# A row-sum kernel on one core: both halves of a row summed at once in the last 16 rows, fewer last loads, big buffers at a multiple of 1 KB

## Chip, cores, metric

One core of one Trainium2 chip. The metric is the device time of one execution in microseconds; a kernel's time is the median of its runs. The profile's span of the same execution is 1.5 us shorter (161.17 and 159.6 us for before).

## The reference

```python
batch, seq, dim = 32, 512, 1024            # x: float32, 64 MB
return (np.sum(x, axis=-1) / divisor).astype(np.float32)     # divisor = 1024.0
```

16,384 rows of 1024 numbers are read once, each row is summed and scaled: 67.11 MB in, 64 KB out. Each of the 128 partitions has 128 rows.

## The kernel before

The rows come in a few large loads on the SyncE queue into three buffers of 14 rows. VectorE sums most rows with a reduction, ScalarE takes some near the end with an accumulating copy into PSUM. The last 16 rows per partition ("the tail") come in smaller and smaller loads, so that little is left to do when the last byte lands. The last row of all comes in three pieces.

```python
first = [(2, 0), (14, 0)]                      # (rows of a load, of them on ScalarE)
main = [(14, 0)] * 5 + [(14, 4), (12, 5)]
last = [(8, 4), (4, 2), (2, 1)]
bulk = ctx.enter_context(tc.tile_pool(name="bulk", bufs=3))
one = ctx.enter_context(tc.tile_pool(name="one", bufs=1))
# ... small result tiles res0, res, fin, q, r

def act_sum(dst, src, by=1.0):                 # ScalarE
    n = src.shape[-1]
    junk = psum.tile([P, D], F32, name="junk")
    nc.scalar.activation(junk[:, :n], src, COPY, scale=by, accum_out=dst)

def sums(dst, t, rows, on_act):
    d = rows - on_act
    for i in range(d, rows):
        act_sum(dst[:, i : i + 1], t[:, i, :])
    nc.vector.reduce_sum(out=dst[:, :d], in_=t[:, :d, :], axis=AX)
# ... first and main: load, sums(), then one scaling on GpSimd
# ... last: load, sums() into q

c = 704                                        # the row before the last: both engines share it
row = one.tile([P, D], F32, name="row")
load(row, x_last[:, j, :])
act_sum(r, row[:, c:], by=scale)
nc.vector.reduce_sum(out=q[:, j : j + 1], in_=row[:, :c], axis=AX)

a, b = 448, 704                                # the last row: three pieces
# ... pa, pb, pc
load(pa, x_last[:, L - 1, :a])
load(pb, x_last[:, L - 1, a:b])
load(pc[:, : D - b], x_last[:, L - 1, b:])
# ... the results of first and main are stored
act_sum(pc[:, D - b : D - b + 1], pa)
nc.vector.reduce_sum(out=pc[:, D - b + 1 :], in_=pb, axis=AX)
# ... two GpSimd instructions scale the other 15 sums into fin
nc.vector.tensor_scalar(
    out=scaled, in0=pc, scalar1=scale, scalar2=0.0, op0=MULT, op1=ADD, accum_out=fin[:, L - 1 :]
)
tc.keep_in_program_order(nc.sync.dma_start(out=o_last, in_=fin))
```

The last store waits for VectorE, and the queue that issues it first waits until every other transfer, the two earlier result stores included, has landed.

## Time and profile before

| | before |
|---|---|
| time, median of 3 runs | 161.13 us (161.07 to 161.52) |
| span of the profiled run | 159.6 us |
| VectorE / ScalarE / GpSimd busy | 120.9 / 19.7 / 1.4 us |
| bytes over the span | 421 GB/s |
| loads | 16, of 128 KB to 7 MB |
| first load landed / last load landed | 4.94 / 157.54 us |
| final store leaves / lands | 158.18 / 159.59 us |

The first column of a timeline or a chain is the time from the start of the span. A load has landed when its last completion event stands in the trace; an engine that waited for it alone starts 0.02 us later. A handover is the time from the end of one instruction to the start of the next one that needs its result. Nearly all of the span is one unbroken stream of loads: from the first landing to the last one of before the DMA share is 0.99 at 427 GB/s, and in the 2.05 us behind it 0.05.

### The profile page before, as it was taken

Reading aid. Unit: us, or ns where it says so; the run is one execution under the profiler, and the core shown is the slowest. Engines: PE = TensorE matmul, PEld = TensorE weight load, DVE = VectorE, ACT = ScalarE, POOL = GpSimd, SP = SyncE. Lnnn points to the kernel's source line nnn. Section 1 sums busy time; section 2 is a strip of 40 time slices with the busy share of each in tenths; the row PEclk is TensorE's granted clock in tenths of the full one; section 3 lists DMA queues with packets and bytes.
Section 4 is the critical chain, followed back from the end, with each engine's and each line's share of the span. In section 5 each row is a group of like instructions: output and inputs, shape, how many; then the busy total and the mean of one; then the engine's idle time right before and its main releaser. Section 6 shows DMA issues by size and latency. Waiting matters only on the chain.

```text
span 159.6 us, 143 instructions
## 1 busy us (share of the span) xinstructions
DVE 120.9 (76%) x16; ACT 19.7 (12%) x37; POOL 1.4 (1%) x8
## 2 busy tenths in 40 slices
DVE  0500059995999599977999599959995996495985
ACT  3000000000000000000000000000000900490974
POOL 0000000000000000000000000000000000001001
DMA  7999999987999999978999999969999999898994
GB/s 253 470 460 460 460 460 460 431 374 345 460 460 460 460 460 460 417 345 388 460 460 460 460 460 460 402 302 445 460 460 427 394 431 542 357 443 378 413 407 133
DMA packets 2736, 67.18 MB, mean 421 GB/s; under 512 B 688, under 2 KB 1072, under 8 KB 1200
## 3 DMA queue, kind: packets, MB, share of 16 engines
q1 hardware_dynamic: 2736, 67.18, 98.0%
HBM read 67.11 MB, written 0.07 MB: 421 GB/s over the span
## 4 chain that ended last, share of the span: by engine, by line
DMA 76%; DVE 22%; SPq 0%; issue 0%; DVEq 0%
DMA t<-in_x_dram 76%; DVE res L159 20%; DVE q L159 1%; DVE q L184 1%; SPq L148 0%; DVE scaled L207 0%; DVE pc L201 0%; DVEq L207 0%; DVEq L241 0%
## 5 line engine op out<-in xcount | busy, mean ns | idle before, releaser
L159 DVE TENSOR_REDUCE res<-t 128x14 f32<-128x14336 f32 (+3 forms) x9 | 111.2, 12360 | 34.4 <-DMA t<-in_x_dram 34.4
L153 ACT ACTIVATE junk<-t 128x1024 f32<-128x1024 f32 x16 | 16.2, 1013 | 136.0 <-DMA t<-in_x_dram 136.0
L159 DVE TENSOR_REDUCE q<-t 128x4 f32<-128x4096 f32 (+2 forms) x3 | 7.9, 2642 | 2.7 <-DMA t<-in_x_dram 2.7
L153 ACT ACTIVATION_READ_ACCUMULATOR junk<-t 128x1 f32 x16 | 3.0, 187 | 0.0
L168 POOL TENSOR_SCALAR res<-res 128x16 f32<-128x16 f32 (+1 forms) x2 | 0.7, 352 | 145.1 <-DVE res L159 145.1
L153 ACT ACT_TABLE_LOAD x1 | 1.3, 1283 | 1.7 <-PEq L227 1.7
L184 DVE TENSOR_REDUCE q<-row 128x1 f32<-128x704 f32 x1 | 0.9, 885 | 0.0
L207 DVE TENSOR_SCALAR_CACHE_REDUCE scaled<-pc 128x322 f32<-128x322 f32 x1 | 0.5, 489 | 0.1
L153 ACT ACTIVATE junk<-pa 128x448 f32<-128x448 f32 x1 | 0.5, 547 | 0.0
L153 ACT ACTIVATE junk<-row 128x320 f32<-128x320 f32 x1 | 0.4, 442 | 0.1
L201 DVE TENSOR_REDUCE pc<-pb 128x1 f32<-128x256 f32 x1 | 0.4, 420 | 0.0
L202 POOL TENSOR_SCALAR fin<-q 128x14 f32<-128x14 f32 x1 | 0.3, 260 | 10.1 <-DVE q L159 10.1
L203 POOL TENSOR_SCALAR fin<-q,r 128x1 f32<-128x1 f32 x1 | 0.3, 265 | 0.7 <-DVE q L184 0.7
L153 ACT ACTIVATION_READ_ACCUMULATOR junk<-pa 128x1 f32 x1 | 0.2, 187 | 0.0
L153 ACT ACTIVATION_READ_ACCUMULATOR junk<-row 128x1 f32 x1 | 0.2, 186 | 0.0
L227 POOL MEMSET const-bfloat16-1.0<- 128x1 bf16 x1 | 0.1, 101 | 0.0
L227 POOL MEMSET const-uint8-127<- 128x1 uint8 x1 | 0.1, 101 | 0.0
L227 POOL MEMSET const-float32-0.0<- 128x1 f32 x1 | 0.1, 98 | 0.2 <-issue 0.2
L227 POOL MEMSET const-float32-1.0<- 128x1 f32 x1 | 0.1, 99 | 0.0
L207 DVE DVE_READ_ACCUMULATOR scaled<-pc 128x1 f32 x1 | 0.1, 82 | 0.0
## 6 DMA issues: line engine op xcount, KB each, us to landing
t<-in_x_dram SPq DMA_DIRECT2D x7, 7168.0 KB, 35.7
t<-in_x_dram SPq DMA_DIRECT2D x1, 6144.0 KB, 33.3
t<-in_x_dram SPq DMA_DIRECT2D x1, 4096.0 KB, 26.1
t<-in_x_dram SPq DMA_DIRECT2D x2, 1024.0 KB, 18.7
t<-in_x_dram SPq DMA_DIRECT2D x1, 2048.0 KB, 30.5
row<-in_x_dram SPq DMA_DIRECT2D x1, 512.0 KB, 33.2
pa<-in_x_dram SPq DMA_DIRECT2D x1, 224.0 KB, 33.3
pc<-in_x_dram SPq DMA_DIRECT2D x1, 160.0 KB, 33.0
```

The costliest lines, as they stand in the source:

```text
L153: nc.scalar.activation(junk[:, :n], src, COPY, scale=by, accum_out=dst)
L159: nc.vector.reduce_sum(out=dst[:, :d], in_=t[:, :d, :], axis=AX)
L168: nc.gpsimd.tensor_scalar_mul(out=dst, in0=dst, scalar1=scale)
L184: nc.vector.reduce_sum(out=q[:, j : j + 1], in_=row[:, :c], axis=AX)
L201: nc.vector.reduce_sum(out=pc[:, D - b + 1 :], in_=pb, axis=AX)
L202: nc.gpsimd.tensor_scalar_mul(out=fin[:, :j], in0=q[:, :j], scalar1=scale)
L203: nc.gpsimd.tensor_scalar(out=fin[:, j : j + 1], in0=q[:, j : j + 1], scalar1=scale, scalar2=r, op0=MULT, op1=ADD)
L207: nc.vector.tensor_scalar(out=scaled, in0=pc, scalar1=scale, scalar2=0.0, op0=MULT, op1=ADD, accum_out=fin[:, L - 1 :])
L227: nc = _bacc.Bacc("TRN2", target_bir_lowering=False, num_devices=1)
```

## The change

The intent is to shorten what is left at the end. Rows of the tail are summed by VectorE with a two-source instruction that reads the left and the right half of a row together, so that 512 steps do for 1024 columns, and that scales its sum, so that no scaling follows. With quicker sums the tail has fewer loads: 9, 4 and 2 rows and the last row in two pieces. A pad puts the big buffers at byte 17408 in place of 16512, a multiple of 1 KB. In the built programs the small tiles of the tail move too, from multiples of 256 B to multiples of 1 KB.

```diff
-    last = [(8, 4), (4, 2), (2, 1)]
+    last = [(9, 4), (4, 2), (2, 1)]
+    pad = ctx.enter_context(tc.tile_pool(name="pad", bufs=1))
+    pad.tile([P, 224], F32, name="pad")
     bulk = ctx.enter_context(tc.tile_pool(name="bulk", bufs=3))
+    c = 576
+    pa = one.tile([P, 768], F32, name="pa")[:, :c]
+    pb = one.tile([P, D - c + 16], F32, name="pb")[:, : D - c + 2]
+    nc.gpsimd.memset(pb[:, D - c :], 0.0)
+    def dve_mean(dst, src, by=scale):
+        h = src.shape[-1] // 2
+        nc.vector.tensor_tensor_reduce(
+            out=src[:, :h], in0=src[:, :h], in1=src[:, h:], scale=by, scalar=0.0,
+            op0=ADD, op1=ADD, accum_out=dst,
+        )
 ...   (tail: per row dve_mean or act_sum straight into fin)
-    load(row, x_last[:, j, :])
-    load(pa, x_last[:, L - 1, :a])
-    load(pb, x_last[:, L - 1, a:b])
-    load(pc[:, : D - b], x_last[:, L - 1, b:])
+    load(pa, x_last[:, j, :c])
+    load(pb[:, : D - c], x_last[:, j, c:])
 ...
-    act_sum(pc[:, D - b : D - b + 1], pa)
-    nc.vector.reduce_sum(out=pc[:, D - b + 1 :], in_=pb, axis=AX)
-    (three more instructions that scale and add)
+    dve_mean(pb[:, D - c : D - c + 1], pa, by=1.0)
+    dve_mean(fin[:, j:], pb)
```

## The prediction

The sum came to about −0.35 us, 160.8 us: −0.3 for the tail and −0.05 booked for the alignment. The point of 160.85 and the range were set with it. The 85 to 15 for the full rate is the author's own estimate, as no VectorE instruction in the trace of before reads two tensors; the full rate, N/0.96 + 152 ns for N columns, is carried over from the reductions in that trace.

> **What bounds the kernel now.** I first read the chain that ended last, to see whether the time is a stream, an engine or a handover. By line it is 76% loads and 20% the first VectorE reduction, and in order of time its end is this:
>
> ```profile
> 122.55 32.46 DMA t<-in_x_dram
> ...
> 155.04 1.22 DVE q L159
> 156.25 0.01 issue
> 156.27 0.89 DVE q L184
> 157.15 0.39 DVE pc L201
> 157.55 0.04 DVEq L207
> 157.58 0.08 issue
> 157.66 0.49 DVE scaled L207
> ```
>
> The load stream reaches to 155.01 us; then come 3.2 us of VectorE on the last three rows, of which only the last 0.6 us lies behind the last byte (the last piece was issued at 124.49 us and landed 33.0 us later, 157.5 us). So only some tenths of a microsecond at the end are not the stream. The 20% of VectorE inside the chain is no bound: each 14-row reduction of 15.09 us frees a buffer while other loads are queued. The table by stage checks that (columns: span, VectorE, ScalarE and GpSimd busy, clock, DMA share, GB/s):
>
> ```profile
> 40.00:80.00 40.00, 36.31 (x3) 0.00 (x0) 0.00 (x0) 1.00 1.00 434
> 80.00:120.00 40.00, 36.28 (x3) 0.00 (x0) 0.00 (x0) 1.00 1.01 436
> ```
>
> The queues are full, at 434 to 436 GB/s. The timeline of VectorE gives the pace and what the tail does (start, length, instruction, then the idle time before it):
>
> ```profile
> 89.63 15.09 DVE L159 TENSOR_REDUCE res<-t 128x14 f32<-128x14336 f32 x1 [1.85 <-DMA t<-in_x_dram]
> 106.58 15.09 DVE L159 TENSOR_REDUCE res<-t 128x14 f32<-128x14336 f32 x1 [1.86 <-DMA t<-in_x_dram]
> ...
> 138.06 7.62 DVE L159 TENSOR_REDUCE res<-t 128x7 f32<-128x7168 f32 x1 [3.72 <-DMA t<-in_x_dram]
> 147.77 4.42 DVE L159 TENSOR_REDUCE q<-t 128x4 f32<-128x4096 f32 x1 [2.09 <-DMA t<-in_x_dram]
> 152.60 2.29 DVE L159 TENSOR_REDUCE q<-t 128x2 f32<-128x2048 f32 x1 [0.41 <-DMA t<-in_x_dram]
> 155.04 1.22 DVE L159 TENSOR_REDUCE q<-t 128x1 f32<-128x1024 f32 x1 [0.15 <-DMA t<-in_x_dram]
> 156.27 0.89 DVE L184 TENSOR_REDUCE q<-row 128x1 f32<-128x704 f32 x1
> 157.12 0.42 DVE L201 TENSOR_REDUCE pc<-pb 128x1 f32<-128x256 f32 x1
> 157.66 0.49 DVE L207 TENSOR_SCALAR_CACHE_REDUCE scaled<-pc 128x322 f32<-128x322 f32 x1
> ```
>
> Every large reduction waits for its load, so VectorE has slack of 1.85 us per 14 rows. Two landings are 16.95 us apart: 7,340,032 bytes, 433 GB/s. From 156.27 us VectorE runs with almost no gap: there it and the stream are level. Last, what the issuing queue waits for before the final store:
>
> ```profile
> SPq L241 <- DMA out_dram<-res: 1.0, 1, 1.0
> ...
> SPq L210 <- DVE scaled L207: 0.2, 1, 0.2
> ```
>
> It also waits for the two earlier result stores (issued 138.10 and 147.81, landing 19.6 and 10.1 us later: 157.7 and 157.9 us), and only then 0.2 us for VectorE. A faster VectorE alone can win those 0.2 us and no more, unless the stream ends earlier too. The final store (158.18 us) takes 1.4 us and ends the span of 159.6; the measured time is 161.13, 1.5 us more.
>
> [...] In the built programs the three big buffers start at byte 16512 before[...] and at 17408 after (a multiple of 1 KB). The trace of before has no aligned big load to compare. [...] In the trace the reductions [...] 885 ns at 704, 1219 at 1024, 4420 at 4096, which is N/0.96 + 152. [...] No instruction of the trace before has two tensor inputs[...]. [...] I take the full rate as likely, 85 to 15.
>
> **The change part by part.** *Bytes and loads.* The same 67.11 MB; 14 loads for 16: 9 rows for 8, then 4, 2, and the last row in two pieces (576 and 448 columns) for a separate row and three pieces. At the pace above (8 rows took 147.77 − 138.06 = 9.71 us, a row 1.21 us), the landings become: 9 rows 148.97, 4 rows 153.8, 2 rows 156.2 (where the separate row landed), first piece (294,912 B at 433 GB/s, 0.68 us) 156.88, second (229,376 B, 0.53 us) 157.41. That is about 0.1 us earlier than 157.5, for two handovers and a small transfer fewer.
>
> [...]
>
> *VectorE.* Removed: a 4-row, a 2-row and a 1-row reduction, 704, 256 and the scaling of 322 columns: 4.42 + 2.29 + 1.22 + 0.89 + 0.42 + 0.49 = 9.73 us. Added at full rate: eight rows of 512 columns, 512/0.96 + 152 = 685 ns, then 288 columns (452 ns) and 225 (386 ns): 6.3 us, and an accumulator read for each (82 ns in the trace, begun 0.41 us into a 0.49 us instruction, so it lies mostly inside). Of these 3.4 us nearly all are beside the stream: five rows end at 152.4, before 153.8; two at 155.2, before 156.2; one at 156.9. Then the first piece, 156.92 to 157.37, and its sum is handed to the last instruction at about 157.42, level with the second piece. The last one runs 157.46 to 157.85. Before, it ended at 158.15: 0.3 us earlier.
>
> *ScalarE.* 4, 2 and 1 rows as before at 1.04 us each; the last ends near 157.4, inside the above. The short sums of 320 and 448 columns (0.44 and 0.55 us) and the two late GpSimd scalings go: they were hidden. An early fill of the two padding columns (101 ns for such an instruction) is hidden too.
>
> *The store.* The two earlier stores are queued behind all loads. They landed 0.4 us behind the last piece (157.9 against 157.5), so 157.8 now, and the final store leaves at about 157.87 instead of 158.18. Sum: −0.3 us[...].
>
> **Rivals.** *Half rate.* Then a row costs 1024/0.96 + 152 = 1219 ns, some 1.2 us start to start: five rows from 148.97 end at 155.0, two at 157.4, one at 158.6, the pieces at 159.3 and 159.9; the store then ends at 161.4, +1.8 us: 162.9. [...] Against: [...] that 5 of 9 rows are given to VectorE and 4 to ScalarE, where 4 and 4 were balanced at 1.07 and 1.01 us a row.
> *The earlier stores take the place of the wait removed.* If they land at 157.9 as before, the gain stops at 0.2 us: 160.9. For it: the 1.0 and 0.2 us above.
> *The end of the stream is a floor.* If the last piece lands at 157.5 and the handover from the first piece's sum costs 0.1 us more, as the 0.08 us of "issue" ahead of the last instruction before hints, the gain is 0.1 to 0.2 us: 161.0.
> [...]
>
> **Range and chances.** I take 160.85, between the sum and the two floors. The runs before span 161.07 to 161.52, so 0.2 us of scatter belongs to any median of three. The range 160.4 to 161.5 has [...] a tail that gains nothing, with scatter, at its high end; half rate lies outside. Faster by 2% would need 3.2 us, more than all that lies behind 155.01 us can give[...]: 0.01. Slower by 2% needs worse than half rate: 0.02. Within 2%: 0.97.
>
> **What would show it.** In the timeline of the changed kernel: the new instruction at 0.68 us for 512 columns (1.2 us is half rate); VectorE idle before the 4-row, the 2-row and the last-piece instruction, each ended by a load; the last load landing at 157.2 to 157.5; final store leaving at 157.8 to 158.0. 14-row landings at 16.9 us or less would credit the alignment; at 16.95 it did nothing. I am wrong if VectorE ends over 0.6 us behind the last landing, or if the landings move by over 0.7 us in all.

## The result, and the profile after

160.69 us (160.63 to 161.28, 6 runs) against 161.10 us (160.92 to 161.52, 6 runs). The ratio is 0.9979 with a 95% interval of 0.9961 to 0.9997: within 2%, inside the predicted range. A ratio is the mean time of one kernel's runs over the mean of the other's of the same rounds, so it is not quite the ratio of the medians quoted. Two later sets of the same kernel gave 0.9987 and 0.9991.

The timeline of VectorE in the kernel after, same columns as in the prediction:

```profile
89.33 15.09 DVE L177 TENSOR_REDUCE res<-t 128x14 f32<-128x14336 f32 x1 [1.81 <-DMA t<-in_x_dram]
106.24 15.09 DVE L177 TENSOR_REDUCE res<-t 128x14 f32<-128x14336 f32 x1 [1.83 <-DMA t<-in_x_dram]
...
148.61 0.69 DVE L164 CUSTOM_DVE_ANT_0 t<-t 128x512 f32<-128x512 f32 x1 [3.25 <-DMA t<-in_x_dram]
149.23 0.08 DVE L164 DVE_READ_ACCUMULATOR2_ANT fin<- 128x1 f32 x1
149.23 0.69 DVE L164 CUSTOM_DVE_ANT_0 t<-t 128x512 f32<-128x512 f32 x1
...
153.46 0.69 DVE L164 CUSTOM_DVE_ANT_0 t<-t 128x512 f32<-128x512 f32 x1 [1.70 <-DMA t<-in_x_dram]
...
155.96 0.69 DVE L164 CUSTOM_DVE_ANT_0 t<-t 128x512 f32<-128x512 f32 x1 [1.19 <-DMA t<-in_x_dram]
156.58 0.08 DVE L164 DVE_READ_ACCUMULATOR2_ANT fin<- 128x1 f32 x1
156.68 0.46 DVE L164 CUSTOM_DVE_ANT_0 pa<-pa 128x288 f32<-128x288 f32 x1
157.06 0.08 DVE L164 DVE_READ_ACCUMULATOR2_ANT pb<- 128x1 f32 x1
157.29 0.40 DVE L164 CUSTOM_DVE_ANT_0 pb<-pb 128x225 f32<-128x225 f32 x1
```

The new instruction takes 0.69 us and the next starts 0.62 us after its start. VectorE now waits for the load ahead of the 4-row and the 2-row tile for 1.7 and 1.2 us, where it waited 0.41 and 0.15 us before. From 155.96 us it runs through to the end with one gap, the handover ahead of its last instruction, as it did before from 156.27 us. The chain that ended last shows the end, in order of time:

```profile
156.68 0.46 DVE pa L164
157.13 0.02 DVE pb L164
157.16 0.03 issue
157.18 0.02 DVEq L164
157.21 0.08 issue
157.29 0.40 DVE pb L164
```

The first piece's sum ends at 157.14 us; 0.15 us later the last instruction starts. The second piece landed at 157.18 us, in between, so this trace alone does not say which of the two came last. The six profiles with this load plan and these sums cut in two pieces do: the start is 0.14 to 0.15 us behind the sum's end in each, whether the piece had landed 0.17 us before that end (experiment 8) or landed 0.05 us after it (experiment 2). So it is the handover from VectorE to itself. The waits of the issuing queue, where the line for the result stores and the one for VectorE stood before:

```profile
SPq L231 <- DMA t<-in_x_dram: 9.7, 1, 9.7
SPq L231 <- DMA pa<-in_x_dram: 0.7, 1, 0.7
SPq L231 <- PEq L231: 0.6, 2, 0.4
SPq L231 <- DMA pb<-in_x_dram: 0.5, 1, 0.5
```

That the two lines are gone means only that these waits are short: by the trace's records, which hold more than the view prints, the queue still waited 0.13 us for each result store and 0.09 us for VectorE.

Where did 0.46 us between the two final stores (158.18 and 157.72 us) come from? I split both traces at landings:

| stretch | before | after | difference |
|---|---|---|---|
| start to first landing | 4.94 | 4.74 | −0.20 |
| first landing to the last of the first 112 rows | 133.09 | 132.98 | −0.11 |
| from there to the landing of 15 of 16 tail rows | 18.21 | 18.22 | 0.00 |
| from there to the final store | 1.94 | 1.78 | −0.16 |

Only the last line is the tail that the change was made for (0.15 us against the mean of three profiles of the kernel after, below). The first two, 0.31 us, are the stream, before any changed sum. Either the alignment of the big buffers made it quicker, or the stream scatters from run to run and the first comparison was lucky.

### The profile page after: what moved, and what is told of

Read it like the earlier page. It is cut to its first block, busy times and chain, and to the rows that moved or that the text cites. A ratio compares the mean times of both kernels' runs of the same rounds, so it can differ in the third digit from the quotient of the medians. Undisturbed runs are those within 1.5% of the kernel's fastest.

```text
span 159.2 us, 147 instructions
## 1 busy us (share of the span) xinstructions
DVE 117.3 (74%) x29; ACT 18.5 (12%) x33; POOL 1.0 (1%) x7
## 4 chain that ended last, share of the span: by engine, by line
DMA 77%; DVE 21%; issue 1%; SPq 0%; DVEq 0%
DMA t<-in_x_dram 77%; DVE res L177 20%; SPq L154 0%; DVE pa L164 0%; DVE pb L164 0%; DVE fin L164 0%; DVE t L164 0%; DVEq L164 0%; DVEq L231 0%
## 5 line engine op out<-in xcount | busy, mean ns | idle before, releaser
L164 DVE CUSTOM_DVE_ANT_0 t<-t 128x512 f32<-128x512 f32 x8 | 5.1, 690 | 6.1 <-DMA t<-in_x_dram 6.1
L164 DVE DVE_READ_ACCUMULATOR2_ANT fin<- 128x1 f32 x9 | 0.7, 83 | 0.0
L164 DVE CUSTOM_DVE_ANT_0 pa<-pa 128x288 f32<-128x288 f32 x1 | 0.5, 459 | 0.0
```

Source lines behind the costliest of these rows:

```text
L164: nc.vector.tensor_tensor_reduce(out=src[:, :h], in0=src[:, :h], in1=src[:, h:], scale=by, scalar=0.0, op0=ADD, op1=ADD, accum_out=dst,)
```

## The experiments

All ratios are to the kernel before on the same chip in the same rounds.

**1. The alignment alone.** The kernel before with its big buffers moved to byte 17408; the small tiles keep their place relative to 256 B.

```diff
+    pad = ctx.enter_context(tc.tile_pool(name="pad", bufs=1))
+    pad.tile([P, 224], F32, name="pad")
-    r = one.tile([P, 16], F32, name="r")[:, :1]
+    r = one.tile([P, 48], F32, name="r")[:, :1]
```

> The kernel before, with its three big buffers moved from byte 16512 to 17408 (a multiple of 1 KB) and nothing else of the change. Theory 1 (the stream came 0.3 us earlier because of the alignment): the first load lands at 4.75 instead of 4.95 us, 14-row landings are 16.92 us apart instead of 16.94, the last load lands near 157.2 us, and the time is 0.2 to 0.35 us below before (ratio 0.998). Theory 2 (the start of the stream differs by chance, the alignment does nothing): landings as before, ratio 1.000 within 0.001.

Measured: 161.49 us (160.88 to 161.84) against 161.13, ratio 1.0008 (0.9986 to 1.0031). The first load did land early, at 4.47 us, but the 14-row landings were 17.07 us apart and the last load landed at 158.24 us. So there was no gain, but with wide scatter, hence a second set of the same kernel later:

> The kernel before with aligned big buffers, once more, since its first set scattered widely (160.88 to 161.84). If the alignment does nothing: ratio 1.000 within 0.001, and the 14-row landings again at 16.94 to 17.0 us. If it costs or gains: the same sign as in the first set (1.0008), or below 0.9985.

Measured: 161.15 us (160.94 to 161.45) against 161.06, ratio 1.0007 (0.9995 to 1.0019). The pace was 16.92 us this time and the first landing 4.71 us: the same program, and a pace 0.16 us per load quicker than in the first set. No gain from alignment in two sets. The first interval leaves room for a gain of 0.14%, the second for 0.05% (0.08 us).

**2. The change without the alignment.** The pad stands behind the big buffers instead of ahead of them.

```diff
-    pad = ctx.enter_context(tc.tile_pool(name="pad", bufs=1))
-    pad.tile([P, 224], F32, name="pad")
+    one.tile([P, 224], F32, name="pad")      # first tile of the pool behind the big buffers
```

> The kernel after, with the big buffers back at byte 16512 (the small tiles stay aligned). Theory 1: loses 0.2 to 0.35 us of its 0.41, so that it is 0.05 to 0.2 us below before (ratio 0.999 to 1.000); last load lands near 157.45. Theory 2: as the kernel after, ratio 0.998, last load near 157.2 but for the scatter of the start.

Measured: 160.92 us (160.69 to 161.08), ratio 0.9984 (0.9969 to 1.0000). That is as good as the kernel after in the same rounds (next). The last load landed at 157.42 us, near theory 1's 157.45, but that of the aligned kernel after in these rounds at 157.49 us. The interval is too wide to refuse theory 1 by this run alone; together with experiment 1 nothing is left that speaks for the alignment as what made the stream earlier.

**3. The kernel after, twice more.** No edit.

> The kernel after once more, in the same rounds as the others: ratio 0.997 to 0.999 to before, about 160.7 us. Theory 1 (alignment) says its first load lands at 4.75 us again; theory 2 (chance) that the first landing scatters between 4.7 and 5.0 us from profile to profile.

Measured: 160.97 us (160.78 to 161.09), ratio 0.9987 (0.9972 to 1.0003); first landing at 4.50 us, 14-row landings 16.97 us apart, last landing at 157.49 us, final store 1.80 us behind the 2-row tile's landing. The first landing was earlier than either theory had said.

> The kernel after a third time, to see what of the 0.41 us of the first comparison is left when the scatter of the stream's start and pace is averaged. From the tail alone (final store 1.78 us behind the landing of the 2-row tile, for 1.93 behind the single row's in the old plan) it should be 0.15 us below before: ratio 0.9985 to 0.9995. If the whole 0.41 us of the first comparison belongs to the change, 0.9975.

Measured: 160.73 us (160.65 to 161.53), ratio 0.9991 (0.9975 to 1.0007); first landing 4.74 us, pace 16.93 us, final store 1.77 us behind the landing. The mean differences of the three sets are 0.34, 0.20 and 0.18 us, so 0.24 us on average. What the tail accounts for (0.15) lies inside the interval of every set, and the 0.41 us of the first medians was high. Taken alone, the two later sets do not tell the gain from zero.

**4. The new loads with one-source sums.** Each dve_mean runs over all columns of its row or piece:

```diff
-        nc.vector.tensor_tensor_reduce(out=src[:, :h], in0=src[:, :h], in1=src[:, h:], ...)
+        nc.vector.tensor_scalar(
+            out=src, in0=src, scalar1=by, scalar2=0.0, op0=MULT, op1=ADD, accum_out=dst
+        )
```

> The loads and tiles of after, but each tail row and each piece is summed by VectorE with the one-source instruction (tensor_scalar with an accumulator, scaled) over all its columns. It costs what half rate would have cost: 1024/0.96 + 152 = 1.22 us a row, about 1.15 us start to start. If the two-source instruction is what makes the new loads work, VectorE becomes the bound of the tail: five rows from 148.6 end at 154.4, two at 156.8, one at 157.9, the pieces of 576 and 450 columns at 158.7 and 159.4, against 157.7 in after: 1.5 to 1.8 us more than after, 162.2 to 162.5. If the tail were bound by the stream alone the time would stay at 160.7.

Measured: 162.50 us (162.21 to 162.99), ratio 1.0086 (1.0067 to 1.0105), 1.5 us above the kernel after in the same rounds. The timeline of VectorE in this kernel has no idle time from the 9-row tile on:

```profile
148.56 1.22 DVE L164 TENSOR_SCALAR_CACHE_REDUCE t<-t 128x1024 f32<-128x1024 f32 x1 [3.23 <-DMA t<-in_x_dram]
149.71 0.08 DVE L164 DVE_READ_ACCUMULATOR t<-t 128x1 f32 x1
...
157.68 0.75 DVE L164 TENSOR_SCALAR_CACHE_REDUCE pa<-pa 128x576 f32<-128x576 f32 x1
...
158.56 0.62 DVE L164 TENSOR_SCALAR_CACHE_REDUCE pb<-pb 128x450 f32<-128x450 f32 x1
```

The last load landed at 157.15 us, as early as in the kernel after, but VectorE was 2 us behind it. In this load plan the two-source sums are needed: at 1.14 us from one row's start to the next, in place of 0.62, VectorE is the bound of the tail. Giving ScalarE more of the rows instead was not tried.

**5. The old loads with two-source sums.** Only the sums of the tail rows in the kernel before are swapped (two-source with scale 1.0 into q, 352 steps for the 704 columns); loads, last instructions and stores stay.

```diff
-        sums(q[:, j : j + rows], t, rows, on_act)
+        (ScalarE rows as before, then for each VectorE row:)
+            dve_sum(q[:, j + i : j + i + 1], t[:, i, :])
-    nc.vector.reduce_sum(out=q[:, j : j + 1], in_=row[:, :c], axis=AX)
+    dve_sum(q[:, j : j + 1], row[:, :c])
```

> The loads, tiles and end of the kernel before, with only the tail rows (4, 2, 1 and the 704 columns of the single row) summed by the two-source instruction. My theory (VectorE in the old load plan was beside the stream, the end is set by the last landing and the fixed instruction behind it): the last row's 256-column sum still waits for its own piece, the last instruction still starts 0.1 us behind the last landing and takes 0.49 us, so the final store leaves 0.64 us behind the last landing as in the two profiles with the old plan, and the ratio to before is 1.000 within 0.001. The rival (the quicker instruction is the gain, whatever the loads): 0.15 to 0.3 us below before.

Measured: 161.07 us (160.90 to 161.19) against 161.06, ratio 0.9998 (0.9984 to 1.0011). The timeline of VectorE in this kernel shows where the saved time went:

```profile
156.31 0.53 DVE L163 CUSTOM_DVE_ANT_0 row<-row 128x352 f32<-128x352 f32 x1 [0.54 <-DMA row<-in_x_dram]
156.75 0.08 DVE L163 DVE_READ_ACCUMULATOR2_ANT q<- 128x1 f32 x1
157.15 0.42 DVE L212 TENSOR_REDUCE pc<-pb 128x1 f32<-128x256 f32 x1 [0.31 <-DMA pb<-in_x_dram]
157.68 0.49 DVE L218 TENSOR_SCALAR_CACHE_REDUCE scaled<-pc 128x322 f32<-128x322 f32 x1
```

It became waiting for loads, 0.54 and 0.31 us of it. The final store leaves 0.64 us behind the last landing, as before (0.65), and 1.92 us behind the separate row's (1.94). That is firmer than the ratio, whose interval leaves room for a gain of 0.16%. Neither half of the change is a gain alone: quicker sums in the old plan gain nothing, the new plan with slow sums loses 1.4 us against before.

**6. A last instruction that is almost free.** It sums 4 columns in place of 450. The result is wrong on purpose in the last row of each partition.

```diff
-    dve_mean(fin[:, j:], pb)
+    dve_mean(fin[:, j:], pb[:, D - c - 2 :])
```

> After with the last instruction summing 4 columns in place of 450 (a wrong result on purpose: the last row of each partition): it takes 154 ns for 396. If nothing but VectorE stands behind the last landing, the final store leaves 0.28 us behind it (0.54 in after). If the two earlier result stores are a floor, as my prediction's second rival had it, it leaves 0.36 to 0.40 us behind it, right after the second of them has landed (0.35 us behind the last load). The time falls by 0.15 to 0.25 us against after, to about 160.6.

Measured: 160.62 us (160.61 to 160.71), ratio 0.9971 (0.9956 to 0.9987). In its timelines of VectorE and of the issuing queue:

```profile
157.35 0.16 DVE L164 CUSTOM_DVE_ANT_0 pb<-pb 128x2 f32<-128x2 f32 x1
...
157.72 0.33 SPq L200 DMA_DIRECT2D out_dram<-fin  x1
```

The last load landed at 157.25 us, VectorE was done at 157.51 us, yet the store left at 157.72 us, 0.47 us behind the last load. So VectorE alone does not set it. The second of the earlier result stores landed at 157.58 us, behind VectorE's end, and the store left 0.14 us behind that. The floor is there, and it lies higher than expected (0.36 to 0.40). The 0.14 us are steps of the issuing queue, which stand in the trace's records though no view prints them: the wait for that store is over at 157.60 us, a drain comes at 157.66, the issue at 157.72. Counted from the 2-row tile's landing the final store leaves at 1.72 us, for 1.78 us in the kernel after: of 0.24 us taken from VectorE only 0.06 us reached the end. The time hit the expected 160.6 us, but no set of the kernel after ran in these rounds, so the stretch in the trace, and not the time, measures this.

**7. The last row in six pieces.**

```diff
-    load(pa, x_last[:, j, :c])
-    load(pb[:, : D - c], x_last[:, j, c:])
+    for k in range(0, c, 192):
+        load(pa[:, k : k + 192], x_last[:, j, k : k + 192])
+    for k, n in ((0, 152), (152, 152), (304, 144)):
+        load(pb[:, k : k + n], x_last[:, j, c + k : c + k + n])
```

> After with the last row brought in six pieces (three of 192 columns, then 152, 152, 144) in place of two; sums unchanged. If each further load costs the stream something at the end (in before, row to last landing was 1.29 and 1.34 us with four loads, in after 1.24 with two), the time from the landing of the 2-row tile to the last landing grows from 1.24 us to 1.33 to 1.6 us, and the whole by as much (0.1 to 0.35 us). If transfers merge in the queue at no cost, it stays at 1.24.

Measured: 161.19 us (161.08 to 161.44), ratio 1.0008 (0.9991 to 1.0024): the gain is gone. From the 2-row tile's landing to the last landing it took 1.41 us in place of 1.24, so 0.04 us for each of four more loads (count and shorter rows together; they are not separated here). It is no constant: the old plan, with one load more behind that landing than the new (three, not the four of the text above), took 0.05 to 0.10 us longer. The final store left 2.17 us behind that landing in place of 1.78, which is more than the landings alone: the first piece's sum now started 0.23 us behind the landing of its last part (it waits for three loads), and the two result stores, issued later because each waited for a load (at 153.61 us, behind a landing at 153.55, and at 156.14, behind 156.08), landed at 157.68 and 157.87 us. VectorE did not come last here: it signalled its end at 158.11 us, but in the trace's records the queue still went through four more waits, all long fulfilled, and a drain, some 0.06 us apart, before it issued the store at 158.25 us. So about 0.1 us of the loss is the order of the queue's own waits.

**8. Another cut of the last row.**

```diff
-    c = 576
+    c = 704
```

> After with the last row cut at 704 columns in place of 576. If the end is a chain on VectorE (row, first piece, handover, second piece), the first piece's sum ends later (landing 0.83 us behind the 2-row tile, 352 columns in 0.52 us, handover 0.15) and the last instruction starts 1.50 us behind the landing of the 2-row tile in place of 1.35, lasts 0.32 in place of 0.40: the final store leaves 0.05 to 0.1 us later than in after, counted from that landing (1.78 us in after). If it is bound by the last landing alone it leaves 0.08 us earlier. The time itself stays within 0.1 us of after, too little for the clock of whole runs.

Measured: 160.82 us (160.75 to 160.89), ratio 0.9984 (0.9966 to 1.0002). The end of its VectorE timeline:

```profile
155.85 0.69 DVE L164 CUSTOM_DVE_ANT_0 t<-t 128x512 f32<-128x512 f32 x1 [1.19 <-DMA t<-in_x_dram]
...
156.73 0.52 DVE L164 CUSTOM_DVE_ANT_0 pa<-pa 128x352 f32<-128x352 f32 x1 [0.17 <-DMA pa<-in_x_dram]
157.18 0.08 DVE L164 DVE_READ_ACCUMULATOR2_ANT pb<- 128x1 f32 x1
157.40 0.33 DVE L164 CUSTOM_DVE_ANT_0 pb<-pb 128x161 f32<-128x161 f32 x1
```

The last load landed at 157.08 us, and the last instruction started 0.32 us later, when the first piece's sum had been handed over. The final store left 1.94 us behind the 2-row tile's landing: 0.16 us later than with 576, more than the 0.05 to 0.1 expected, in part because the larger first piece also landed later (0.88 us for an expected 0.83) and VectorE had to wait for it. So the end is a chain on VectorE, and at 576 the first piece lands just as VectorE is done with the last full row. No version here that gives right results is shown to be faster than the kernel after: the two best ratios, 0.9984 here and in experiment 2, lie among its own (0.9979, 0.9987, 0.9991).

**The profiles side by side** (those of experiments 6 to 8 stand in their text; all us: landing of the first load; distance of 14-row landings, mean of six; from the landing of 15 of 16 tail rows to the last landing and to the final store):

| kernel | first | pace | to last landing | to final store |
|---|---|---|---|---|
| before | 4.94 | 16.94 | 1.29 | 1.94 |
| before, aligned (two sets) | 4.47, 4.71 | 17.07, 16.92 | 1.34, 1.34 | 1.96, 1.95 |
| before, two-source sums | 4.95 | 16.94 | 1.29 | 1.92 |
| after (three sets) | 4.74, 4.50, 4.74 | 16.92, 16.97, 16.93 | 1.24, 1.24, 1.24 | 1.78, 1.80, 1.77 |
| after, not aligned | 4.48 | 16.99 | 1.24 | 1.76 |
| after, one-source sums | 4.51 | 16.94 | 1.25 | 3.32 |

The first two columns scatter by 0.5 us and by 0.16 us per load without regard to the kernel: all four kernels of the first batch started at 4.5 us, and one and the same program had both the slowest and the quickest pace. The last two columns are steady, and they separate the two load plans by 0.05 to 0.1 us and by 0.12 to 0.2 us.

## Why the prediction was right

**The bound.** Right: the stream is the time, and all that the change can touch is behind the landing of the last full row. The stretch of the tail up to that landing took 18.21 and 18.22 us in the two traces. It is not free of scatter: in the second set's profile of the kernel after it took 18.41 us.

**The rate of the new instruction.** Right, at the estimate of 85 to 15: 690 ns measured for 685 at 512 columns, 459 for 452 at 288, 396 for 386 at 225. With the 0.16 us for 2 columns in experiment 6 that is 1.04 ns a step of two columns. The rival of half rate was made to happen with other means (experiment 4): 1.5 us more than the full rate. The rival's own figure, 162.9 us, compares with 162.5 us.

**The tail's sum, term by term**, counted from the landing of the last full row (156.2 in the prediction):

| | before | predicted | after |
|---|---|---|---|
| last landing | 1.29 | 1.21 | 1.24 |
| last VectorE instruction starts | 1.41 | 1.26 | 1.35 |
| it ends | 1.90 | 1.65 | 1.75 |
| final store leaves | 1.94 | 1.67 | 1.78 |

Fewer pieces gained 0.05 us of the expected 0.1, the shorter last instruction 0.09 of 0.10. Mis-sized was the handover: the prediction has the first piece's sum end at 157.37 and the last instruction start at 157.46, 0.09 us later. It took 0.15 us, as the third rival had warned from the 0.08 us of issue time in the chain before. The rest is small: the last landing came 0.03 us later than the sum had it. And 0.05 us of the −0.3 was rounding: the sum for the new plan counts from 156.2 us, where the landing it stands for was at 156.25. So the tail gave 0.15 us and not 0.3.

**The alignment.** Booked at 0.05 us. Two sets with it alone (1.0008 and 1.0007) and one of the change without it (0.9984) show no gain from it.

**The total came out near for a mixed reason.** Predicted 160.85 us, measured 160.69 in the first set, 160.97 and 160.73 later: the prediction lies among them. In the profile that was compared first, that is luck: 0.15 us of the tail and 0.31 us of the stream make up the 0.46 us, where the sum had 0.3 and 0.05. Against before the point stood for 0.28 us, and the mean of three sets is 0.24. Of this, 0.15 us is shown in the tail; the remaining 0.1 us is within the scatter of the stream, and no run tells it from zero.

**Its own signs.** The instruction's 0.69 us and the waits ahead of the 4-row and the 2-row tile came as said. The other three did not: the last landing, 157.18 us, and the final store, 157.72 us, lay before the windows of 157.2 to 157.5 and 157.8 to 158.0, as the stream was 0.31 us early, and the last instruction waited for VectorE, not for a load. The sign for the alignment, landings at 16.9 us or less, was of no use: the measured 16.92 us lay between its two figures, and the pace scatters by 0.16 us. (The 436 GB/s of one window of before comes with a DMA share of 1.01, so a window is good to about 1%.)

**The earlier stores.** The rival put their floor at a gain of 0.2 us. The trace of before puts it lower: there the queue's drain ended at 158.00 us, and with the 0.05 us from drain to issue of experiment 6 the store could have left at about 158.05 us, an estimated gain of 0.13. In the kernel after they landed at 157.53 us, behind which VectorE's end at 157.69 us still came last. Experiment 6 shows the floor 0.06 us below: further work on the last instruction would have run into it.

What stays open: why the start and the pace of the stream differ from run to run, whether the last 0.1 us of the mean gain is the change's, and what the new places of the small tiles do.

## What to carry to other kernels

When one stream of loads fills the time, count from landings: what mattered here was the stretch from the last large landing to the final store (1.94 us before, 1.78 after), and a quicker instruction gained there only as far as it came last: of 0.24 us taken from the last one in experiment 6, 0.06 us reached the end. Quicker sums and fewer, larger last loads were worth something only together; each alone gave nothing (0.9998) or a loss (1.0086). And compare kernels by intervals of the trace that do not scatter before believing a difference of 0.3% between medians.
